# Triangles inverted as 64x64 blocks, a third set of a pair's prepared tiles, and another list of the weave

## The chip, the cores and the metric

The kernel runs on one core of one Trainium2 chip. The metric is the device time of one execution in microseconds (us); a time is the median of the timed executions. The core has a matrix engine (TensorE, PE in the rows), a vector engine (VectorE, DVE), a scalar engine (ScalarE, ACT), a general engine (GpSimd, POOL) and a sync engine (SP) that issues most of the transfers. Each engine works through a list of instructions of its own, in that list's order.

## What is computed

Two blocks of a model on 256 tokens of width 1024. The change touches one part of the first block, the RWKV-7 recurrence, which runs over the tokens in both directions. Beside it, in the same stage, stand an attention with eight heads and the output projection of both.

```python
def wkv7_scan(r, w, k, v, kk, a, reverse):          # per head: S is 64 x 64
    def step(state, inp):
        r_t, w_t, k_t, v_t, kk_t, a_t = inp
        sa = jnp.einsum('bhvk,bhk->bhv', state, -kk_t)
        state = (state * w_t[:, :, None, :]
                 + sa[..., :, None] * (kk_t * a_t)[..., None, :]
                 + v_t[..., :, None] * k_t[..., None, :])
        y = jnp.einsum('bhvk,bhk->bhv', state, r_t)
        return state, y

def first_block(...):
    mod = silu(c) @ ada_w + ada_b          # six modulation vectors
    ...
    att = dilated_mixture_attention(qa, ka, va).reshape(B, S, A)
    rw = rwkv7_bidirectional(...)          # wkv7_scan, forward and reversed, 8 heads
    mixed = jnp.concatenate([att, rw], axis=-1) @ w_out
    x = x + gate1 * mixed
    ...
```

## The kernel before

The recurrence is computed in chunks of 64 tokens. In a chunk the sequential steps are a triangular system, whose matrix is inverted by doubling: a triangle made of blocks is put together from inverses half as large, in five levels. What is left between chunks is a chain of 64x64 states.

Two heads make a **pair**, so there are four pairs, 0 to 3 (class `Pair`). A pair has two directions `d` and two halves `t` of the tokens; a half has two chunks of 64. For each pair five kinds of tasks are written as Python generators:

- `prepare` (its products stand at L606 to L670 of the profile) makes what the recurrence needs of a pair: `vn`, `na`, `nbk`, `ar`, `btk`, `az`, `bon`. The names come from the helpers `t1` and `t2`, which add `q % 2` to most of them, so that there are two sets of these tiles, used by pairs in turn.
- `start(d, t)` (L687) makes the chunk's products of tokens with tokens and masks them (L691, L693) into `PR`. `PR` holds, for two heads and two matrices, 128x128 matrices that are zero outside their two diagonal 64x64 blocks, one block for each chunk. `PB` is a copy for the last sums; it too has two sets.
- `tile(d, t)` is the inversion. GpSimd makes the first `X` (L708, L709) from `MA`, the system's matrix in `PR`. Each of five levels has two **half-levels**: two products with `MA` on TensorE (L720) and a multiplication with a mask, `PP`, on VectorE (L721), then two products with `PP` (L725), a transpose on VectorE (L727) and a copy on an engine that is free (L728). All of these are 128x128 for each head. Three products (L735, L743, L746) give `W`.
- `states` (L761 to L774) is the chain over the four chunks in both directions, and ends with 16 sums into `y` (L595, from `PB` and `W`).
- `finish` (L789 to L804) normalises `y` and writes the pair's output.

The function `weave` puts the tasks of the stage into one order: pairs 0 to 3, the eight attention heads (L522 to L553, one after the other, since all use one tile `bias`), the modulation vectors that are needed later (`ada`: VectorE's multiply-adds L341, 1024 KB of weights each load, and sums on TensorE at L345), and the output projection (`outs`: splits of the weights at L99 and L100, three products at L106 to L108, additions to x at L954). It keeps an estimate of when each engine is free and each task ready, takes the task that could start first, and among equals the one that stands first in the list. It starts when pair 0 is prepared; the other pairs' `prepare` stands in the list with what it must follow. `prepare` of pair q waits for all of `start` of pair q - 1 and for `finish` of pair q - 2, whose tiles it writes over:

```python
first.append((("pre", q), pairs[q].prepare(), tuple(("s", q - 1, d, t) for d in range(2) for t in range(2))
              + ((("fin", q - 2),) if q > 1 else ())))
```

Behind the weave stand the fourth pair's part of the output projection, a loop over the last weights that were loaded ahead (the first products at L106 from `zr` and `kk`), and then the rest of the first block and the second block.

Of the kernel before, what the change touches and what calls it, by code (L numbers as in the profile page):

```python
# [28 lines left out]
HALVES = slice(0, 64), slice(64, 128)  # L29
# [409 lines left out]
def masks(k, keep, pool):  # L439
# [10 lines left out]
    up = pool.tile([128, 128], F, name="up")  # L450
    nc.vector.tensor_tensor(up, pi, fi, op=OP.is_lt)
    lo = pool.tile([128, 128], F, name="lo")
    nc.vector.tensor_tensor(lo, pi, fi, op=OP.is_gt)
    m = keep.tile([128, 2, 8, 128], F, name="masks")
    t = pool.tile([128, 128], F, name="mt")
    for d, tri in enumerate((up, lo)):
        nc.vector.scalar_tensor_tensor(m[:, d, 6], xf, 64.0, tri, op0=OP.is_lt, op1=OP.mult)
        nc.vector.tensor_tensor(m[:, d, 7], m[:, d, 6], k.ident, op=OP.add)
        for i in range(6):
# [3 lines left out]
            nc.vector.tensor_tensor(m[:, d, i], m[:, d, i], k.ident, op=OP.add)  # L463
    k.masks = m
    k.bm = keep.tile([128, 128], F, name="bm")
    nc.vector.tensor_scalar(k.bm, xf, 64.0, None, op0=OP.is_lt)
# [103 lines left out]
class Pair:  # L570
# [8 lines left out]
    def t1(self, name):  # L579
        keep = name[:2] in ("vn", "na", "kd", "bo")  # L580
        return self.pool.tile([128, T], F, name=name + (str(self.q % 2) if keep else ""))

    def t2(self, name, shape):
        return self.pool.tile(shape, F, name=name + (str(self.q % 2) if name[:3] != "btk" else ""))
# [13 lines left out]
    def prepare(self):  # L598
# [75 lines left out]
        self.W, self.PB = [None] * 2, [[None] * 2 for _ in range(2)]  # L674

    def start(self, d, t):
# [4 lines left out]
        PR = self.blocks(pool, f"PR{d}{t}", [128, 2, 2, 2, 128])  # L681
# [7 lines left out]
        for x in range(2):  # L689
            for r in HALVES:  # L690
                nc.vector.tensor_tensor(PR[r, :, x, :, r], ps[x][r], up[r, None, 6:8, r].to_broadcast([64, 2, 2, 64]),  # L691
                                        op=OP.mult)
        nc.gpsimd.tensor_copy(self.PB[d][t], PR[:, :, 0, 1])  # L693

    def tile(self, d, t):
# [6 lines left out]
        bc = lambda x: x[:, None, :].to_broadcast([128, 2, 128])  # L702
        PR = k.zeroed[f"PR{d}{t}"]
        X = pool.tile([128, 2, 2, 128], F, name=f"X{d}{t}")
        pp = pool.tile([128, 2, 128], F, name=f"PP{d}{t}")
        MA = PR[:, :, 0, 0]

        nc.gpsimd.tensor_tensor(MA, MA, bc(k.ident), op=OP.add)  # L708
# [1412 lines left out]
```

## Time and profile before

| | us |
|---|---|
| median of 3 timed executions | 2327.96 (2327.71 to 2334.68) |
| the profiled execution | 2320.28 |
| its span, first to last instruction | 2318.2 |
| TensorE busy | 2191.8 (95% of the span) |
| VectorE busy | 1735.9 (75%) |
| ScalarE busy | 1264.6 (55%) |
| GpSimd busy | 809.6 (35%) |
| mean granted TensorE clock | 0.973 |

A row of a timeline tells when instructions of one kind started on an engine, for how long they ran, the line of the kernel, the operation, the tile written and the tiles read, the instruction's shape and how many rows like it were put together. Matrix products overlap, so the time from one start to the next is what one costs, and the time in the row is that with its latency. A row of a group tells the busy time in all, the mean ns of one, the idle time ahead of them, and what ended most of it. The granted clock is the share of full speed that TensorE was given.

### The profile page before, as it was taken

Reading aid. Unit: us, or ns where it says so; the run is one execution under the profiler, and the core shown is the slowest. Engines: PE = TensorE matmul, PEld = TensorE weight load, DVE = VectorE, ACT = ScalarE, POOL = GpSimd, SP = SyncE. Lnnn points to the kernel's source line nnn. Section 1 sums busy time; section 2 is a strip of 40 time slices with the busy share of each in tenths; the row PEclk is TensorE's granted clock in tenths of the full one; section 3 lists DMA queues with packets and bytes.
Section 4 is the critical chain, followed back from the end, with each engine's and each line's share of the span. In section 5 each row is a group of like instructions: output and inputs, shape, how many; then the busy total and the mean of one; then the engine's idle time right before and its main releaser. Section 6 shows DMA issues by size and latency. Waiting matters only on the chain.

```text
span 2318.2 us, 46849 instructions
## 1 busy us (share of the span) xinstructions
PE 2191.8 (95%) x17962; PEld 2079.0 (90%) x17962; DVE 1735.9 (75%) x3278; ACT 1264.6 (55%) x2689; POOL 809.6 (35%) x811
## 2 busy tenths in 40 slices
PE   6999898789899999999999999899999999989998
PEld 3878587789799999999999999878899999979998
DVE  6888886899877888777776765678875666777664
ACT  3543532735477776555554644447556666536543
POOL 1132320569877777444444100101432221131000
PEclk8999898899999999999999999999999999989999
DMA  7422123447655666666665675323565555516663
GB/s 266 149 92 86 61 73 96 119 107 173 162 148 155 154 150 177 196 196 195 193 193 165 185 219 193 122 74 111 155 202 166 181 162 191 178 36 192 190 200 119
DMA packets 304064, 358.38 MB, mean 155 GB/s; under 512 B 24188, under 2 KB 276576, under 8 KB 302816
## 3 DMA queue, kind: packets, MB, share of 16 engines
q1 hardware_dynamic: 291456, 349.53, 50.0%
q10 hardware_dynamic: 12384, 5.86, 1.0%
q8 instruction: 141, 2.31, 0.4%
q14 instruction: 83, 0.68, 0.1%
HBM read 354.28 MB, written 1.05 MB: 153 GB/s over the span
## 4 chain that ended last, share of the span: by engine, by line
PE 76%; DVE 13%; DMA 3%; ACT 3%; issue 2%; POOL 2%; SPq 0%; ACTq 0%; DVEq 0%; POOLq 0%
PE g L106 12%; PE g L108 12%; PE g L107 12%; PE o L106 4%; PE o L107 4%; PE o L108 3%; PE g L1162 2%; PE y L1314 2%; PE o L1314 2%; PE y L1312 2%; PE o L1312 2%; PE o L1313 2%; PE y L1313 2%; DVE uT L1001 2%; DVE wl L100 2%
## 5 line engine op out<-in xcount | busy, mean ns | idle before, releaser
L99 ACT ACTIVATE wh<-raw 128x1024 fp32r<-128x1024 f32 (+3 forms) x397 | 387.1, 977 | 389.2 <-PE g L107 185.5
L100 DVE TENSOR_TENSOR wl<-raw,wh 128x1024 fp32r<-128x1024 f32 (+3 forms) x381 | 431.6, 1135 | 223.2 <-ACT wh L99 209.8
L106 PE MATMUL g<-xh,wh 128*128 128x256 f32 x1864 | 529.9, 285 | 8.7 <-ACT xh L374 5.8
L108 PE MATMUL g<-xh,wl 128*128 128x256 f32 x1864 | 525.4, 282 | 8.4 <-DVE wl L100 8.3
L107 PE MATMUL g<-xl,wh 128*128 128x256 f32 x1864 | 524.6, 282 | 4.1 <-DVE xl L375 2.7
L1001 POOL TENSOR_TENSOR ul<-uT,uh 128x512 fp32r<-128x512 f32 x320 | 411.6, 1306 | 188.4 <-ACT uh L1001 188.4
L106 PEld LDWEIGHTS g<-xh,wh 128*128 128x128 f32 x1864 | 357.5, 192 | 15.2 <-ACT xh L374 6.9
L108 PEld LDWEIGHTS g<-xh,wl 128*128 128x128 f32 x1864 | 356.2, 191 | 12.1 <-DVE wl L100 11.7
L107 PEld LDWEIGHTS g<-xl,wh 128*128 128x128 f32 x1864 | 356.4, 191 | 6.1 <-DVE xl L375 3.5
L1001 ACT ACTIVATE uh<-uT 128x512 fp32r<-128x512 f32 x384 | 221.3, 627 | 146.5 <-POOL ul L1001 76.5
L108 PE MATMUL g<-ph,ul 128*128 128x256 f32 x1024 | 291.1, 284 | 7.7 <-POOL ul L1001 7.6
L106 PE MATMUL g<-ph,uh 128*128 128x256 f32 x1024 | 292.8, 286 | 3.7 <-ACT uh L1001 2.0
L107 PE MATMUL g<-pl,uh 128*128 128x256 f32 x1024 | 289.1, 282 | 0.0
L108 PEld LDWEIGHTS g<-ph,ul 128*128 128x128 f32 x1024 | 194.7, 190 | 11.3 <-POOL ul L1001 11.1
L106 PE MATMUL o<-hh,wh 128*128 128x256 f32 x704 | 197.8, 281 | 1.6 <-DVE t L1374 1.6
L106 PEld LDWEIGHTS g<-ph,uh 128*128 128x128 f32 x1024 | 195.1, 191 | 4.6 <-ACT uh L1001 2.3
L107 PE MATMUL o<-hl,wh 128*128 128x256 f32 x704 | 197.4, 280 | 0.0
L108 PE MATMUL o<-hh,wl 128*128 128x256 f32 x704 | 197.1, 280 | 0.0
L107 PEld LDWEIGHTS g<-pl,uh 128*128 128x128 f32 x1024 | 195.3, 191 | 0.0
L1001 DVE TENSOR_TENSOR al<-G,ah 128x256 fp32r<-128x256 f32 x128 | 173.9, 1359 | 17.2
L154 POOL TENSOR_TENSOR sql<-sq,sqh 128x256 fp32r<-128x256 f32 x48 | 48.8, 1018 | 340.1 <-ACT sqh L153 336.0
L1001 DVE STREAM_TRANSPOSE uT<-u 128x1024 f32<-128x1024 f32 x128 | 157.8, 1235 | 2.3 <-DMA u<-in_peer_u_dram 1.9
(772 smaller groups left out, 5456.4 us busy)
## 6 DMA issues: line engine op xcount, KB each, us to landing
u<-in_peer_u_dram SPq DMA_DIRECT2D x512, 128.0 KB, 2.6
raw<-in_ffn_w_gate_dram SPq DMA_DIRECT2D x44, 1024.0 KB, 5.6
raw<-in_ffn_w_up_dram SPq DMA_DIRECT2D x44, 1024.0 KB, 5.3
u<-in_peer_v_dram SPq DMA_DIRECT2D x64, 512.0 KB, 4.3
uT<-in_peer_v_dram SPq DMA_DIRECT2D x64, 512.0 KB, 4.2
raw<-in_ffn_w_down_dram SPq DMA_DIRECT2D x32, 1024.0 KB, 5.1
raw<-in_ada_w_dram SPq DMA_DIRECT2D x24, 1024.0 KB, 5.2
raw<-in_w_in_dram SPq DMA_DIRECT2D x13, 1024.0 KB, 5.7
```

What stands on the lines that cost most here:

```text
L99: nc.scalar.activation(h, v, AF.Copy)
L100: self.sub.tensor_tensor(l, v, h.bitcast(F), op=OP.subtract)
L106: nc.tensor.matmul(out, sh, mh, start=first, stop=False)
L107: nc.tensor.matmul(out, sh, ml, start=False, stop=False)
L108: nc.tensor.matmul(out, sl, mh, start=False, stop=last)
L154: self.sub.tensor_tensor(l, sq, h.bitcast(F), op=OP.subtract)
L1001: return lambda *args, **kw: self.tc.keep_in_program_order(f(*args, **kw))
L1162: nc.tensor.matmul(p[:, t], g[:, t], b[:, t], start=True, stop=True)
L1312: nc.tensor.matmul(o, vh[:, s], ah, start=i == 0 and c % 2 == 0, stop=False, skip_group_check=True)
L1313: nc.tensor.matmul(o, vh[:, s], al, start=False, stop=False, skip_group_check=True)
L1314: nc.tensor.matmul(o, vl[:, s], ah, start=False, stop=i == NB - 1, skip_group_check=True)
```

## The change

Three edits. The triangles are now stored as 64x64 blocks: the rows 0 to 63 of a tile hold one chunk's block and the rows 64 to 127 the other's, and the zero blocks are gone. A half-level is four products of 64x64 by 64, two heads times two diagonal quarters of TensorE, in place of two of 128x128 by 128. Masks, `PP`, `X`, transposes and copies are half as wide. `start` writes `PA` (two matrices in blocks) and `PR` (two with zeros, as before); the last level's result is put into `TT`, with zeros, in two copies. Second, `t1` and `t2` name three sets, and `prepare` of pair q waits for `finish` of q - 3; `start` of pair q now waits for `finish` of q - 2, since `PB` and `W` keep two sets. Third, the weave's list has the pairs' tasks first, then the heads, then the modulation.

```diff
     def t1(self, name):
         keep = name[:2] in ("vn", "na", "kd", "bo")
-        return self.pool.tile([128, T], F, name=name + (str(self.q % 2) if keep else ""))
+        return self.pool.tile([128, T], F, name=name + (str(self.q % 3) if keep else ""))
...
+        self.PA[d][t] = PA = pool.tile([128, 2, 2, 64], F, name=f"PA{d}{t}")
+        PR = self.blocks(pool, f"PR{d}{t}", [128, 2, 2, 128])
         self.PB[d][t] = pool.tile([128, 2, 128], F, name=f"PB{d}{t}{self.q % 2}")
...
         for x in range(2):
+            nc.vector.tensor_tensor(PA[:, x], ps[x][:, :, 0], up[:, 6, None].to_broadcast([128, 2, 64]), op=OP.mult)
+        for x in range(2):
             for r in HALVES:
-                nc.vector.tensor_tensor(PR[r, :, x, :, r], ps[x][r], up[r, None, 6:8, r].to_broadcast([64, 2, 2, 64]),
-                                        op=OP.mult)
-        nc.gpsimd.tensor_copy(self.PB[d][t], PR[:, :, 0, 1])
+                nc.vector.tensor_tensor(PR[r, x, :, r], ps[x][r, :, 1], up[r, 7, None].to_broadcast([64, 2, 64]), op=OP.mult)
+        nc.gpsimd.tensor_copy(self.PB[d][t], PR[:, 0])
...
+        ic = [(i, r) for i in range(2) for r in HALVES]
...
         for lv in range(1, 6):
             yield
-            p = k.pw([128, 2, 128])
-            for i in range(2):
-                nc.tensor.matmul(p[:, i], MA[:, i], X[:, 1, i], start=True, stop=True)
+            p = k.pw([128, 2, 64])
+            for i, r in ic:
+                nc.tensor.matmul(p[r, i], MA[r, i], X[r, 1, i], start=True, stop=True)
             nc.vector.tensor_mul(pp, p, bc(lo[:, lv]))
             yield
-            p = k.pw([128, 2, 128])
-            for i in range(2):
-                nc.tensor.matmul(p[:, i], pp[:, i], X[:, 0, i], start=True, stop=True)
+            p = k.pw([128, 2, 64])
+            for i, r in ic:
+                nc.tensor.matmul(p[r, i], pp[r, i], X[r, 0, i], start=True, stop=True)
             if lv < 5:
                 nc.vector.transpose(X[:, 1], p)
-            nc.any.tensor_copy(X[:, 0], p)
+                nc.any.tensor_copy(X[:, 0], p)
+        for r in HALVES:
+            nc.any.tensor_copy(tt[r, :, r], p[r])
...
-                                  + ((("fin", q - 2),) if q > 1 else ())))
+                                  + ((("fin", q - 3),) if q > 2 else ())))
...
                     first.append((("s", q, d, t), pairs[q].start(d, t), ((("pre", q),) if q else ())
-                                  + (((q - 1, d, t),) if q else ())))
+                                  + (((q - 1, d, t),) if q else ()) + ((("fin", q - 2),) if q > 1 else ())))
...
-            weave(nc, ada + heads + first + last + outs + [("ow", last_weights(), ("oa", ("pre", 3)))])
+            weave(nc, first + last + heads + ada + outs + [("ow", last_weights(), ("oa", ("pre", 3)))])
```

The order of instructions moves with it. In what follows a row is the line, the operation, the tile written, the tiles read and how many of the kind follow each other; `x4` of 64x64 is one half-level.

TensorE in the first level of pair 0, before. L720 and L725 are half-levels, L546 and L552 an attention head, L654, L659 and L614 pair 1's `prepare`.

```order
L720 MATMUL o_1717<-X_1635,PR_1581 128x128 x2
L546 MATMUL g_1721<-ident,sc 128x128 x4
L552 MATMUL g_1731<-bias,vna 64x256 x2
L659 MATMUL g_1749<-ident,ar_1703 128x128 x2
L720 MATMUL g_1753<-X_1639,PR_1590 128x128
L654 MATMUL o_1742<-ident,btk_1710 128x128 x4
L720 MATMUL g_1753<-X_1639,PR_1590 128x128
L725 MATMUL o_1757<-X_1635,PP_1636 128x128 x2
```

The same place now (L735 and L740 are the half-levels, L663 and L668 `prepare`).

```order
L735 MATMUL g_1726<-X_1642,PA_1580 64x64 x4
L735 MATMUL o_1732<-X_1648,PA_1590 64x64 x4
L735 MATMUL g_1738<-X_1654,PA_1607 64x64 x4
L740 MATMUL g_1744<-X_1642,PP_1643 64x64 x4
L740 MATMUL o_1751<-X_1648,PP_1649 64x64 x4
L740 MATMUL g_1758<-X_1654,PP_1655 64x64 x4
L663 MATMUL g_1766<-ident,btk_1712 128x128 x4
L668 MATMUL o_1773<-ident,ar_1705 128x128 x2
```

Half-levels of three tiles follow each other directly, and no attention head stands between them.

TensorE around `finish` of pair 0 and `start` of pair 2, now (L807, L812 and L818 are `finish`, L698 is `start`; L750 to L761 are the products for `W` of pair 1).

```order
L807 MATMUL o_2642<-y,bm 128x256
L740 MATMUL g_2646<-X_2102,PP_2103 64x64 x4
L735 MATMUL g_2653<-X_2366,PA_2270 64x64 x4
L750 MATMUL g_2670<-vn_1674,PA_2072 64x64 x4
L812 MATMUL o_2659<-sq,bm 128x256
L740 MATMUL g_2676<-X_2366,PP_2367 64x64 x4
L758 MATMUL o_2687<-PP_2103,TT_1656 128x64 x2
L761 MATMUL o_2687<-TT_1656,na_1772 64x128 x2
L818 MATMUL g_2693<-lora_378,gup 128x256
L698 MATMUL g_2698<-az_1128,btk_2340 64x256 x2
L698 MATMUL o_2699<-az_1128,btk_2340 64x256 x2
```

Before, pair 2's `prepare` (L606, L614) stood behind the last product of pair 0's `finish` (L803), and 38 rows lay between that and its `start`.

```order
L803 MATMUL g_2523<-lora_372,gup 128x256
L606 MATMUL g_2527<-ident,zr_369 128x128 x2
L614 MATMUL g_2535<-lora_371,wda 128x256
L720 MATMUL g_2539<-X_2192,PR_1620 128x128 x2
L743 MATMUL o_2517<-PP_2133,X_2132 128x64 x2
```

Now `start` itself stands directly behind it, and pair 2's `prepare` ahead.

TensorE behind the last pair's sums, before.

```order
L595 MATMUL y_3244<-PB_3360,W_3629 64x128 x2
L595 MATMUL y_3244<-PB_3220,W_3629 64x128 x2
L792 MATMUL g_4081<-y,bm 128x256
L803 MATMUL g_4096<-lora_372,gup 128x256
L797 MATMUL o_4085<-sq,bm 128x256
L106 MATMUL g_4109<-zr_4105,kk 128x256
L107 MATMUL g_4109<-zr_4106,kk 128x256
```

The same place now (L536, L555 and L561 are attention heads, L345 the modulation).

```order
L604 MATMUL y_3281<-PB_3464,W_3697 64x128 x2
L604 MATMUL y_3281<-PB_3247,W_3697 64x128 x2
L555 MATMUL o_3977<-ident,sc 128x128 x4
L807 MATMUL g_3984<-y,bm 128x256
L561 MATMUL o_4005<-bias,vna 64x256 x2
L812 MATMUL g_3988<-sq,bm 128x256
L345 MATMUL g_3999<-one,acc 128x1 x4
L818 MATMUL g_4012<-lora_378,gup 128x256
L536 MATMUL g_4019<-qk_385,qk_381 128x256 x2
L555 MATMUL o_4040<-ident,sc 128x128 x4
L561 MATMUL g_4048<-bias,vna 64x256 x2
L345 MATMUL g_4055<-one,acc 128x1 x4
```

Before, the loop over the last weights (L106) followed `finish`; now heads 4 to 7, the last five of the modulation's eight groups and 168 products of the output projection stand between.

VectorE in one of these heads, now (L538, L541, L542, L548, L550 and L562 are the head's steps, L341 the modulation's multiply-adds).

```order
L538 TENSOR_TENSOR sc<-g_4111,bias 128x512
L341 SCALAR_TENSOR_TENSOR acc<-raw,ct,acc 128x512
L541 TENSOR_REDUCE smx<-sc 128x2
L341 SCALAR_TENSOR_TENSOR acc<-raw,ct,acc 128x512
L542 TENSOR_SCALAR smx<-smx 128x2
L341 SCALAR_TENSOR_TENSOR acc<-raw,ct,acc 128x512 x2
L548 RECIPROCAL sden<-sden 128x2
L341 SCALAR_TENSOR_TENSOR acc<-raw,ct,acc 128x512
L550 TENSOR_SCALAR sc<-sc,sden 128x256 x2
L562 COPY att<-g_4140 64x256
```

Before, the recurrence's steps stood between the steps of a head.

## Rows read from the trace of the kernel before

**Rows 1.** Busy us by stretch (instructions) of each engine, clock, DMA share, GB/s

```profile
240.00:300.00 60.00, 49.59 (x323) 36.84 (x323) 53.00 (x140) 29.05 (x70) 24.01 (x24) 0.89 0.14 45
...
372.00:400.00 28.00, 22.73 (x141) 17.53 (x140) 15.16 (x40) 5.08 (x11) 0.00 (x0) 0.81 0.34 107
sum 260.00, PE 237.53 PEld 191.84 DVE 218.95 ACT 102.20 POOL 64.50; mean PE 59.38 PEld 47.96 DVE 54.74 ACT 25.55 POOL 16.12
```

**Rows 2.** Timeline of TensorE, half-levels and a head: start us, us, instruction

```profile
301.47 0.71 PE L720 MATMUL g<-X,PR 128*128 128x128 f32 x4
302.02 0.61 PE L720 MATMUL o<-X,PR 128*128 128x128 f32 x4
302.47 1.06 PE L720 MATMUL g<-X,PR 128*128 128x128 f32 x8
303.36 0.60 PE L670 MATMUL o<-kd,bm 128*128 128x256 f32 x2
303.79 0.38 PE L725 MATMUL g<-X,PP 128*128 128x128 f32 x2
```

**Rows 3.** Timeline of TensorE, two products of a start

```profile
307.85 0.60 PE L687 MATMUL o<-az,btk 128*64 128x256 f32 x4
308.28 0.60 PE L687 MATMUL g<-az,btk 128*64 128x256 f32 x4
```

**Rows 4.** Timeline of TensorE, two products in a prepare

```profile
279.27 0.48 PE L614 MATMUL o<-lora,wda 64*128 64x256 f32 x1
279.27 0.48 PE L614 MATMUL g<-lora,wda 64*128 64x256 f32 x1
```

**Rows 5.** Timeline of TensorE in the second block

```profile
1501.45 0.28 PE L106 MATMUL g<-xh,wh 128*128 128x256 f32 x1
1501.56 0.28 PE L107 MATMUL g<-xl,wh 128*128 128x256 f32 x1
1501.76 0.29 PE L1523 MATMUL o<-cg,w 64*64 64x15 f32 x4
1501.98 0.60 PE L119 MATMUL o<-one,R 1*128 1x1 f32 x4
```

**Rows 6.** Groups of VectorE, 140 to 350 us: busy us, mean ns | idle before

```profile
L341 DVE SCALAR_TENSOR_TENSOR acc<-raw,ct,acc 128x512 f32<-128x512 f32 x44 | 34.1, 775 | 0.1
L721 DVE TENSOR_TENSOR PP<-g,masks 128x256 f32<-128x256 f32 x49 | 19.9, 412 | 4.2 <-PE g L720 3.5
L727 DVE STREAM_TRANSPOSE X<-g 128x256 f32<-128x256 f32 x39 | 16.5, 432 | 2.5 <-PE g L725 2.4
...
L532 DVE TENSOR_REDUCE smx<-sc 128x2 f32<-128x512 f32 x8 | 5.3, 668 | 0.0
...
L772 DVE TENSOR_TENSOR st<-sn,g 128x128 f32<-128x128 f32 x10 | 2.7, 275 | 1.3 <-PE g L768 1.2
```

**Rows 7.** Timeline of TensorE: pair 0's sums, pair 2's prepare and start

```profile
226.14 1.04 PE L595 MATMUL y<-PB,W 128*64 128x128 f32 x16
...
233.85 0.38 PE L606 MATMUL g<-ident,zr 128*128 128x128 f32 x2
...
258.23 0.65 PE L687 MATMUL o<-az,btk 128*64 128x256 f32 x4
```

**Rows 8.** Groups of GpSimd, 140 to 350 us

```profile
L522 POOL TENSOR_SCALAR bias<-df 128x512 f32<-128x512 f32 x7 | 11.7, 1676 | 38.5 <-PE g L552 38.4
L523 POOL TENSOR_TENSOR bias<-bias,lc 128x512 f32<-128x512 f32 x8 | 10.9, 1358 | 0.3
```

**Rows 9.** Groups of ScalarE, 140 to 350 us

```profile
L537 ACT ACTIVATE sc<-sc,smx 128x256 f32<-128x256 f32 x16 | 8.0, 500 | 3.6 <-DVE smx L533 3.5
L548 ACT COPY bias<-g 128x512 f32<-128x512 f32 x6 | 3.5, 586 | 7.9 <-PE g L546 7.9
```

**Rows 10.** The chain that ended last, 387 to 411 us: start us, us, what

```profile
389.39 2.39 PE y L595 x18
...
399.92 0.58 PE g L106
```

More of the change, by code (lines that the diff above doesn't have):

```diff
@@ L449, in masks @@
     nc.vector.tensor_copy(xf, xi)
[L450 to L455, printed above, removed]
+    k.bm = keep.tile([128, 128], F, name="bm")
+    nc.vector.tensor_scalar(k.bm, xf, 64.0, None, op0=OP.is_lt)
+    pc = pool.tile([128, 64], I32, name="pc")
+    nc.vector.tensor_scalar(pc, pi[:, 0:64], 63, None, op0=OP.bitwise_and)
+    fc = fi[:, 0:64]
+    xi, xf = xi[:, 0:64], xf[:, 0:64]
+    nc.vector.tensor_tensor(xi, pc, fc, op=OP.bitwise_xor)
+    nc.vector.tensor_copy(xf, xi)
+    up = pool.tile([128, 64], F, name="up")
+    nc.vector.tensor_tensor(up, pc, fc, op=OP.is_lt)
+    lo = pool.tile([128, 64], F, name="lo")
+    nc.vector.tensor_tensor(lo, pc, fc, op=OP.is_gt)
+    m = keep.tile([128, 2, 8, 64], F, name="masks")
+    k.unit = keep.tile([128, 64], F, name="unit")
+    nc.vector.tensor_tensor(k.unit, pc, fc, op=OP.is_equal)
+    t = pool.tile([128, 64], F, name="mt")
     for d, tri in enumerate((up, lo)):
-        nc.vector.scalar_tensor_tensor(m[:, d, 6], xf, 64.0, tri, op0=OP.is_lt, op1=OP.mult)
-        nc.vector.tensor_tensor(m[:, d, 7], m[:, d, 6], k.ident, op=OP.add)
+        nc.vector.tensor_copy(m[:, d, 6], tri)
+        nc.vector.tensor_tensor(m[:, d, 7], tri, k.unit, op=OP.add)
         for i in range(6):
@@ L462, in masks @@
             nc.vector.scalar_tensor_tensor(m[:, d, i], xf, 2 * b, t, op0=OP.is_lt, op1=OP.mult)
-            nc.vector.tensor_tensor(m[:, d, i], m[:, d, i], k.ident, op=OP.add)
+            nc.vector.tensor_tensor(m[:, d, i], m[:, d, i], k.unit, op=OP.add)
     k.masks = m
-    k.bm = keep.tile([128, 128], F, name="bm")
-    nc.vector.tensor_scalar(k.bm, xf, 64.0, None, op0=OP.is_lt)
 def selectors(k, pool):
@@ L580, in t1 @@
         keep = name[:2] in ("vn", "na", "kd", "bo")
-        return self.pool.tile([128, T], F, name=name + (str(self.q % 2) if keep else ""))
+        return self.pool.tile([128, T], F, name=name + (str(self.q % 3) if keep else ""))
     def t2(self, name, shape):
-        return self.pool.tile(shape, F, name=name + (str(self.q % 2) if name[:3] != "btk" else ""))
+        return self.pool.tile(shape, F, name=name + (str(self.q % 3) if name[:3] != "btk" else ""))
     def blocks(self, pool, name, shape):
@@ L673, in prepare @@
         self.yp = None
-        self.W, self.PB = [None] * 2, [[None] * 2 for _ in range(2)]
+        self.W, self.PB, self.PA = [None] * 2, [[None] * 2 for _ in range(2)], [[None] * 2 for _ in range(2)]
     def start(self, d, t):
@@ L701, in tile @@
         up, lo = m[:, d], m[:, 1 - d]
[L702 to L708, printed above, removed]
+        bc = lambda x: x[:, None, :].to_broadcast([128, 2, 64])
+        PR, PA = k.zeroed[f"PR{d}{t}"], self.PA[d][t]
+        X = pool.tile([128, 2, 2, 64], F, name=f"X{d}{t}")
+        pp = pool.tile([128, 2, 64], F, name=f"PP{d}{t}")
+        tt = self.blocks(pool, f"TT{d}{t}", [128, 2, 128])
+        MA = PA[:, 0]
+        ic = [(i, r) for i in range(2) for r in HALVES]
+        nc.gpsimd.tensor_tensor(MA, MA, bc(k.unit), op=OP.add)
         nc.gpsimd.tensor_tensor(X[:, 0], MA, bc(up[:, 0]), op=OP.mult)
@@ L714, in tile @@
             r = slice(64 * i, 64 * i + 64)
[L715 removed]
+            self.ymm(i, self.yp[r, t * 128:(t + 1) * 128], self.vn[:, t, r], PR[:, 1, i])
         for lv in range(1, 6):
             yield
[L718 to L720 removed]
+            p = k.pw([128, 2, 64])
+            for i, r in ic:
+                nc.tensor.matmul(p[r, i], MA[r, i], X[r, 1, i], start=True, stop=True)
             nc.vector.tensor_mul(pp, p, bc(lo[:, lv]))
             yield
[L723 to L725 removed]
+            p = k.pw([128, 2, 64])
+            for i, r in ic:
+                nc.tensor.matmul(p[r, i], pp[r, i], X[r, 0, i], start=True, stop=True)
             if lv < 5:
                 nc.vector.transpose(X[:, 1], p)
[L728 removed]
+                nc.any.tensor_copy(X[:, 0], p)
+        for r in HALVES:
+            nc.any.tensor_copy(tt[r, :, r], p[r])
         yield
[L730 to L731 removed]
+        z0 = pp.rearrange("p i t -> p (i t)")
         p = k.pw([128, 128])
[L733 to L735 removed]
+        for i, r in ic:
+            nc.tensor.matmul(p[r, HALVES[i]], PA[r, 1, i], self.vn[r, t, HALVES[i]], start=True, stop=True)
         nc.any.tensor_copy(z0, p)
```

7 lines of the change are left out of this document (removed).

## The prediction, made before the changed kernel was timed

> **What bounds the kernel now.** I read the busy time by stretches first, then the single rows of the stretch that the change rewrites, then the order of both kernels there. The part in question runs from 140 us, where the first pair's `start` opens the weave, to 399.9 us, where the loop over the last weights opens [rows 1, 10]. In these 260 us TensorE is busy for 237.5 and VectorE for 219.0 (84%); ScalarE (102) and GpSimd (64) bound nothing [rows 1]. There are two weak places. Between 240 and 300 us TensorE is busy for 49.6 of 60 us at a mean granted clock of 0.89, since pair 2 can't start: pair 0's last sums are issued at 226.1, pair 2's `prepare` begins only at 233.9, behind pair 0's `finish`, and its `start` comes at 258.2 [rows 7]. And from 372 on the last pair's states run as a chain of single steps: the clock is at 0.81 and VectorE is busy for 15 of 28 us [rows 1]. What lies behind 400 us is the same code in both kernels, and what lies ahead of 140 loses some mask columns on VectorE while the start waits for weights; I cost both at nothing.
>
> **The change, part by part.**
>
> *Levels of the inversion on TensorE.* There are 16 tiles x 5 levels x 2 = 160 half-levels. Each was two products of 128x128 by 128 columns, which the trace shows as four instructions; now it is four of 64x64 by 64 columns, or eight instructions, which alternate between the two diagonal quarters of the array. Before, one takes 302.47 - 302.02 = 0.45 us from start to start [rows 2]. For the new form the trace has bounds only. If the quarters take turns: four instructions with 64x64 weights, all in one quarter, took 0.22 us, 0.055 each [rows 5], and eight make 0.44, no gain. If the two quarters run at once: 0.22. Halves do run at once here in two rows. Four instructions of 256 columns into the two halves of the output take 0.43 us [rows 3], as long as two do on the whole array [rows 2]; and two products from the two halves of the input start at the same 279.27 us [rows 4]. No row shows the diagonal. I take 0.22, since a diagonal differs in both halves: 160 x 0.23 = 37 us less on TensorE. It comes back in part: a half-level behind other work costs some 0.1 us more (0.55 us from 301.47 to 302.02, against 0.45 [rows 2]), and the new order has about 73 runs of half-levels between instructions of other shapes, so + 7.
>
> *One tile for both quarters.* The two quarters of a half-level write the upper and the lower partitions of one tile `p`; the two products of [rows 4], which start together, write two tiles, `o` and `g`. So no row shows two halves of the input that write one tile at once. If they can't, a half-level takes 0.44 us and not 0.22; that is rival A. The Trainium skill (TensorEngine Tiling (Array Packing), Restrictions and Gotchas) says that different row tiles can't access the same PSUM bank simultaneously, and by that rule A is the case.
>
> *VectorE.* 80 mask products go from 256 to 128 columns: 0.41 us now [rows 6], 0.275 for a product of that width from PSUM [rows 6]; the transposes (64 between levels, 16 ahead of them) from 0.43 to some 0.29. That is 160 x 0.135 = 21.5 us less. `start` has six products of about 0.28 for four of 0.42, the same sum. ScalarE's copies and GpSimd's two steps per tile halve too; neither engine is on the path.
>
> *The third set.* `prepare` of pair 2 now needs `start` of pair 1 and no `finish`. That takes away the wait of [rows 7]: up to the 24 us between 233.9 and 258.2, for pair 2 and again for pair 3. But `PB` and `W` still have two sets, so `start` of pair q now waits for `finish` of q - 2. The order has pair 0's last `finish` product directly ahead of pair 2's `start`. The wait isn't gone, it is shortened to the sums and the four steps of `finish`, while pair 1's levels have TensorE.
>
> *The list.* With the recurrence first, TensorE's order holds attention heads 0 to 2 and the scores of head 3 inside the recurrence; heads 4 to 7, five of the eight modulation groups and all of the out-projection come behind it. So the stage falls into two parts, which I sum apart.
>
> Part I, 140 us to the last sums of pair 3. By TensorE: 237.5, less 168 products of the out-projection at 0.115 [rows 5] = 19.4, less 4.3 heads of (0.86 + 0.45 + 0.86, by the distances of [rows 2]) = 9.3, less some 5 for the sums of five modulation groups (an estimate), less 37, plus 7: 174, so an end at 314 if TensorE never idles; with half of the 22 us that it idles now, 325. By VectorE: 219, less 40 multiply-adds of modulation at 0.775 = 31, less 4.3 heads at 2.3 (add and maximum at 0.67 [rows 6] and five small steps of 0.2) = 10, less 16 splits and 16 adds of the out-projection at 0.67 and 0.41 (by rows of equal width [rows 6]) = 17, less pair 3's `finish`, some ten steps of 0.28, 3, less 21.5, plus 1 for new copies: 137, and at today's 84% 163, so an end at 303. I take 313: the first 35 us (one pair's levels alone) are bound by the chain of steps and the rest by TensorE, and the low-clock stretches go with the wait.
>
> Part II, from there to the loop over the last weights. It is a chain, since the heads share one `bias` tile, which GpSimd fills only when the head before has read it. One head: bias 1.68 + 1.36 on GpSimd [rows 8], add and maximum 0.67 each [rows 6], two exponentials at 0.5 and the copy 0.59 [rows 9], four transposes 0.61 and the product 1.06 with their latency [rows 2], and six small steps (negation, two sums, reciprocal, two scalings), narrower than the 0.28 of [rows 6], at an estimated 0.2 each: 8.8. Between the steps VectorE's order has multiply-adds of the next modulation group: three of the eight lie ahead of a step that is ready, 3 x 0.775 = 2.3; three lie under GpSimd's bias and two under the exponentials. With ten hand-overs between engines, an estimated 0.8 in all, this is 12 us. The loads of modulation weights that the order has in a head fit under it. Head 3's rest 3, heads 4 to 7 48, the last head's two copies 1.3. Then the out-projection: 168 x 0.115 = 19.4 on TensorE, while VectorE has 17 + 12 multiply-adds at 0.775 = 26; I take 24, since the second half has none of them. Sum: 76.3.
>
> 313 + 76.3 = 389 against 399.9: **11 us less**. The profiled execution took 2320.3 us (span 2318.2); against the median of 2328.0 the same difference gives **2317 us**.
>
> **Rivals.**
>
> A. *The quarters take turns* (ends on the other side). A half-level stays at 0.44, and the new switches stay. Of the 37 us the part that TensorE bounds is behind the first pair, three quarters: + 27. 313 becomes 340, the loop over the last weights starts at 416, 16 us later than now: **2344 us**. It decides from 0.22 + 11 / 120 = 0.31 us a half-level. For it: one tile, and no row with a diagonal. Against it: [rows 3] has two output halves of one tile written at once, and the diagonal's halves share neither input nor output lines.
>
> B. *The tail eats the gain.* Today's attention costs nothing, because it lies beside the levels; in part II TensorE works for about 3 us in 12, and at half the clock, as in the stretch from 372 on [rows 1], a head's transposes and products take 1.3 us more; a late weight load stops VectorE's queue, and the scalings behind it, for another 0.7, about one multiply-add. Four heads then take 56, the out-projection 26.6: + 10.6, and the stage ends where it does now: **2328 us**, no change. For it: every step of the chain is in order. Against it: a share of one head is still beside pair 3's states.
>
> C. *Part I follows VectorE*, 303: 22 us less, **2306 us**. For it: 84% is what VectorE holds over the whole stage [rows 1]. Against it: 314 by TensorE's sum alone.
>
> D. *The wait for `finish` two pairs back replaces the one removed in full*: pair 2 starts 8 us later than the sum supposes, the time from 226.1 to 233.9 in [rows 7], and pair 3 as well; half is filled with pair 1's levels: + 8, **2325 us**.
>
> **How the numbers follow.** The forecast (0.22 us, 12 us a head) has 0.42, A 0.22, B 0.18, C 0.10, D 0.08. About 0.3%, 7 us, is what a measurement of this kernel tells from no change. The forecast's own range is 2308 to 2325, 0.37 of it below 2321; with C that makes 0.47 for faster. B and D and the forecast's upper end make 0.25 for no change; A, with the upper end of B, 0.28 for slower. The range reaches from C with a shorter tail, 2302, to A with some of B on top, 2346; left out are A with all of B and a gain over 1.1%.
>
> **What would show it.** A half-level: the distance from start to start of the new 64x64 rows of lines 735 and 740 where several follow each other, 0.22 or 0.44 us. VectorE's rows of 128x128 at 0.28 to 0.30. Pair 2's `start` near 210 us (258 now), pair 3's sums ending near 313 (some 9 us ahead of 399.9 now), with no stretch below a clock of 0.9 between 180 and 300. Behind it four heads 12 us apart, GpSimd's bias to GpSimd's bias, with a low granted clock, then 24 us of out-projection, and the loop over the last weights at 389. The prediction is wrong if the quarters take turns, if heads lie over 14 us apart, or if part I ends outside 303 to 325.

## The result: slower by 0.9%, and the profile after

The changed kernel takes 2353.2 us (median of 6, 2343.7 to 2358.2) against 2330.1 (median of 6): a ratio of 1.0088, 95% interval 1.0065 to 1.0111, some 20 us slower. 2317 was forecast. The profiled execution took 2354.8 us. It lies 1.6 us above its median and that of before 10 us below its own, so some 11 of the 34 us between the two profiles are not the change. All that follows is read from the stage itself, from the first `start` to the loop over the last weights: 289 us now (141.8 to 430.9), 260 before (140.3 to 399.9).

Busy time by stretches of the kernel after: the recurrence up to pair 3's last sums, the heads behind it, the output projection (columns as in [rows 1]).

```profile
141.80:344.10 202.30, 182.56 (x2132) 134.52 (x2132) 149.68 (x482) 75.04 (x210) 41.82 (x69) 0.87 0.06 20
344.10:403.00 58.90, 30.93 (x103) 19.89 (x103) 37.94 (x74) 15.24 (x36) 11.02 (x8) 0.56 0.46 149
403.00:430.90 27.90, 24.77 (x178) 23.69 (x178) 21.94 (x41) 8.82 (x15) 0.10 (x1) 0.89 0.42 138
```

Part I, forecast to take 173 us, takes 202, and part II 87 in place of 76. A mean clock of 0.87 is some 51 us at the lower level, 1.2 GHz, in part I. They lie in six stretches, two of them of 17 us, the others of 3 to 7. The first long one, in windows of 2 us:

```profile
196.00:198.00 2.00, 1.55 (x30) 1.11 (x26) 2.00 (x6) 1.08 (x3) 0.74 (x1) 1.00 0.03 8
198.00:200.00 2.00, 0.80 (x6) 0.62 (x6) 2.00 (x8) 1.14 (x3) 0.00 (x0) 1.00 0.00 0
200.00:202.00 2.00, 2.00 (x19) 1.11 (x20) 0.62 (x3) 1.74 (x6) 0.00 (x0) 0.77 0.00 0
202.00:204.00 2.00, 2.00 (x27) 1.88 (x26) 1.42 (x5) 1.34 (x5) 0.00 (x0) 0.50 0.00 0
...
218.00:220.00 2.00, 2.00 (x30) 1.37 (x28) 1.03 (x4) 0.10 (x1) 1.92 (x2) 0.96 0.00 0
```

VectorE is busy without a gap from 196 to 200, nearly all of it with pair 2's `prepare`, TensorE waits 1.65 us for its `btk`, and just behind that the clock falls and stays at 0.50 until 218, though TensorE is busy all the time. The same comes back at 249 to 266 with pair 3's `prepare`, where the wait is 1.27 us. Before, heads and modulation stood in these places.

The half-level itself is what was forecast. TensorE's timeline at the full clock (x8 is one half-level; each of its four products is two instructions):

```profile
314.75 0.45 PE L740 MATMUL o<-X,PP 64*64 64x64 f32 x8
315.03 0.40 PE L735 MATMUL g<-X,PA 64*64 64x64 f32 x8
315.26 0.40 PE L750 MATMUL o<-vn,PA 64*64 64x64 f32 x8
...
317.21 0.44 PE L761 MATMUL g<-TT,na 128*64 128x128 f32 x4
317.57 0.45 PE L735 MATMUL g<-X,PA 64*64 64x64 f32 x8
317.95 0.48 PE L807 MATMUL o<-y,bm 128*128 128x256 f32 x1
```

From 315.03 to 315.26 is 0.23 us. The eight instructions behind that row start in pairs, 0.007 us apart in a pair and 0.058 from pair to pair, so the two quarters run at once, though they write one tile. The Trainium skill (TensorEngine Tiling (Array Packing), Restrictions and Gotchas) says that different row tiles can't access one PSUM bank simultaneously; the measurement decides, and by it rival A falls. Alone between other shapes a half-level takes 317.95 - 317.57 = 0.38 us, 0.15 more, where 0.1 was put.

The heads behind the recurrence, by GpSimd's first step of each, which opens a head:

```profile
346.84 1.49 POOL L531 TENSOR_SCALAR bias<-df 128x512 f32<-128x512 f32 x1 [13.07 <-PE o L561]
361.32 1.49 POOL L531 TENSOR_SCALAR bias<-df 128x512 f32<-128x512 f32 x1 [11.64 <-PE g L561]
374.47 1.49 POOL L531 TENSOR_SCALAR bias<-df 128x512 f32<-128x512 f32 x1 [10.31 <-PE g L561]
388.60 1.49 POOL L531 TENSOR_SCALAR bias<-df 128x512 f32<-128x512 f32 x1 [11.29 <-PE g L561]
```

They lie 14.5, 13.2 and 14.1 us apart; 12 was forecast. VectorE's timeline in one of them:

```profile
362.99 0.16 DVE L346 TENSOR_TENSOR mod<-g,V 128x4 f32<-128x4 f32 x1 [3.85 <-PE g L345]
363.08 1.37 DVE L339 TENSOR_SCALAR acc<-raw,ct 128x512 f32<-128x512 f32 x1
364.48 0.75 DVE L341 SCALAR_TENSOR_TENSOR acc<-raw,ct,acc 128x512 f32<-128x512 f32 x1
365.15 0.68 DVE L538 SCALAR_TENSOR_TENSOR sc<-g,bias 128x512 f32<-128x512 f32 x1
365.75 0.74 DVE L341 SCALAR_TENSOR_TENSOR acc<-raw,ct,acc 128x512 f32<-128x512 f32 x1
366.41 0.68 DVE L541 TENSOR_REDUCE smx<-sc 128x2 f32<-128x512 f32 x1
367.00 0.74 DVE L341 SCALAR_TENSOR_TENSOR acc<-raw,ct,acc 128x512 f32<-128x512 f32 x1
367.66 0.16 DVE L542 TENSOR_SCALAR smx<-smx 128x2 f32<-128x2 f32 x1
367.78 1.54 DVE L341 SCALAR_TENSOR_TENSOR acc<-raw,ct,acc 128x512 f32<-128x512 f32 x2
369.23 0.16 DVE L548 RECIPROCAL sden<-sden 128x2 f32<-128x2 f32 x1
369.35 0.75 DVE L341 SCALAR_TENSOR_TENSOR acc<-raw,ct,acc 128x512 f32<-128x512 f32 x1
370.02 0.61 DVE L550 TENSOR_SCALAR sc<-sc,sden 128x256 f32<-128x256 f32 x2
```

Heads and modulation are one chain here. VectorE waits 3.85 us for the sums of the modulation on TensorE (L345), which stand behind the last head's product; then seven of a group's eight steps (L339, L341) stand ahead of the head's scaling (L550), some 5.5 us. Not all of that lengthens the head, since the first of them lie beside GpSimd's bias and two beside the exponentials; how much it does is read from g2 below. TensorE's transposes and last product in the same head:

```profile
370.42 1.16 PE L555 MATMUL o<-ident,sc 128*128 128x128 f32 x4 [5.47 <-DVE sc L550]
372.34 1.97 PE L561 MATMUL g<-bias,vna 128*64 128x256 f32 x4 [0.75 <-ACT bias L557]
```

The clock is at 0.5 here. The prediction had 0.61 and 1.06 for them, at the full clock, so 1.5 us of the head are the clock's. In the output projection TensorE stands still once, behind a split that waits for a load of weights:

```profile
416.09 0.57 PE L106 MATMUL g<-qk,wh 128*128 128x256 f32 x1 [2.92 <-ACT wh L99]
```

### The profile page after: what moved, and what is told of

It reads as the page before. It is cut to its first block, busy times and chain, and to the rows that moved or that the text cites. A ratio compares the mean times of both kernels' runs of the same rounds, so it can differ in the third digit from the quotient of the medians.

```text
span 2353.0 us, 48360 instructions
## 1 busy us (share of the span) xinstructions
PE 2196.0 (93%) x18666; PEld 2066.7 (88%) x18666; DVE 1723.1 (73%) x3331; ACT 1261.7 (54%) x2691; POOL 797.1 (34%) x815
## 4 chain that ended last, share of the span: by engine, by line
PE 75%; DVE 13%; DMA 3%; issue 3%; POOL 2%; ACT 2%; SPq 0%; ACTq 0%; DVEq 0%; POOLq 0%
PE g L106 12%; PE g L108 12%; PE g L107 11%; PE o L106 3%; PE o L107 3%; PE o L108 3%; PE g L1177 2%; PE y L1327 2%; PE o L1327 2%; PE o L1328 2%; PE y L1328 2%; PE o L1329 2%; PE y L1329 2%; DVE uT L1016 2%; DVE wl L100 2%
## 5 line engine op out<-in xcount | busy, mean ns | idle before, releaser
L106 PE MATMUL g<-xh,wh 128*128 128x256 f32 x1864 | 530.1, 285 | 5.5 <-ACT xh L374 2.7
L106 PEld LDWEIGHTS g<-xh,wh 128*128 128x128 f32 x1864 | 356.6, 192 | 11.7 <-ACT xh L374 3.3
L106 PE MATMUL g<-ph,uh 128*128 128x256 f32 x1024 | 292.5, 286 | 3.4 <-ACT uh L1016 1.9
L106 PE MATMUL o<-hh,wh 128*128 128x256 f32 x704 | 197.6, 281 | 1.6 <-DVE t L1389 1.6
L106 PEld LDWEIGHTS g<-ph,uh 128*128 128x128 f32 x1024 | 195.2, 191 | 4.4 <-ACT uh L1016 2.3
```

The costliest lines, as they stand in the source:

```text
L106: nc.tensor.matmul(out, sh, mh, start=first, stop=False)
```

## The three edits apart

Each kernel is given by its edit against the kernel before or after; ratios are to the kernel before, with 95% intervals.

**e1_blocks_third_oldlist**: the kernel after with the list of before.

```diff
-            weave(nc, first + last + heads + ada + outs + ...
+            weave(nc, ada + heads + first + last + outs + ...
```

> The changed kernel with the list of before (modulation, heads, then the recurrence); blocks and third set stay. Theory L (the list costs the time: without heads and modulation in it, TensorE idles in the recurrence behind VectorE, its granted clock falls to 0.5 for 18 us twice, and the heads left over stand alone behind it at 0.5): faster than before by 8 to 20 us, about 2315, and the loop over the last weights opens near 385 us of the profile; between the first start and that loop TensorE is at 0.5 for less than 25 us. Theory B (the 64x64 products cost it, since a half-level between products of other shapes takes 0.38 us and not 0.23, and TensorE's load falls): no faster than before, 2330 or more, and the clock falls here too.

Measured: 2339.3 us, 1.0032 (1.0018 to 1.0047). **e2_blocks_only** takes the sets and waits of before as well (`q % 3` to `q % 2`, `fin` of q - 2 for `prepare`, none for `start`).

> The kernel before with the 64x64 blocks alone: two sets, the waits and the list of before. Theory L: faster than before by some 5 to 12 us, 2320; a half-level takes 0.23 us behind another and some 0.35 elsewhere, where it took 0.45. Theory B: 2330 to 2345, with more low clock than before's 16 us between 240 and 300.

Measured: 2332.6 us, 1.0019 (0.9999 to 1.0038). **e3_list_only** is the kernel before with the new list.

> The kernel before with the new list alone: 128x128 products, two sets. Theory L: slower than before by 15 to 30 us, 2345 to 2360, with heads at 13 to 14 us each behind the recurrence at a clock of 0.5 to 0.6. Theory B: within 7 us of before, 2330.

Measured: 2377.8 us, 1.0206 (1.0183 to 1.0229). **e4_third_only** is the kernel before with three sets and their waits.

> The kernel before with the third set alone (prepare of pair q waits for finish of q - 3, start of pair q for finish of q - 2), 128x128 products and the old list. Theory L: 0 to 8 us faster, 2326: pair 2's prepare comes ahead of pair 0's finish, and the 16 us at a low clock between 240 and 300 shrink, but start still waits for that finish. Theory B makes no other forecast here; if this is slower than before by over 5 us, the third set is a cause of its own.

Measured: 2327.8 us, 0.9984 (0.9972 to 0.9997). **g4_blocks_newlist_two_sets** is the kernel after without the third set.

> The changed kernel (2353 us) without the third set: blocks and the new list, two sets, prepare of pair q behind finish of q - 2 again. If the third set brings what the new list costs less with it (e3_list_only 2378 against 2353 for all three), this takes 2365 to 2378; if the blocks bring it, 2350 to 2358.

Measured: 2358.0 us, 1.0132 (1.0105 to 1.0158), at the upper end of its second case.

So the list costs 2.1% on the kernel before, and still 0.6% with the other two edits (1.0032 to 1.0088). The third set brings 0.2% in the old list with 128x128 products and nothing there with the blocks (e2 to e1); in the new list it brings some 0.4%, but the intervals of g4 and the kernel after overlap. The blocks bring 0.7% under the new list (e3 to g4), but nothing under the old one (0.2% slower with two sets, 0.5% with three). The first part of theory L held, its forecast for e1 and e2 missed, and theory B's was met: narrow products don't pay even with the list of before. The stage of the kernel before and that of e1 show why one may suspect the clock:

```profile
140.30:399.90 259.60, 237.16 (x1705) 191.74 (x1704) 218.56 (x549) 102.20 (x258) 64.20 (x77) 0.94 0.23 73
143.10:419.30 276.20, 244.82 (x2410) 181.14 (x2409) 196.92 (x579) 96.08 (x274) 52.06 (x79) 0.80 0.22 70
```

0.80 in 276 us is 110 us at the lower level; before it was 0.94 in 260, or 31 us. And in e1 it falls where TensorE has no gap at all:

```profile
190.00:192.00 2.00, 2.00 (x29) 1.47 (x27) 1.69 (x4) 0.41 (x2) 0.13 (x1) 1.00 0.01 4
192.00:194.00 2.00, 2.00 (x24) 1.68 (x23) 1.19 (x7) 1.34 (x6) 0.58 (x2) 1.00 0.87 208
194.00:196.00 2.00, 2.00 (x14) 1.27 (x12) 1.96 (x7) 0.48 (x3) 0.66 (x2) 0.66 0.85 325
196.00:198.00 2.00, 2.00 (x10) 1.22 (x6) 0.62 (x3) 0.00 (x0) 0.00 (x0) 0.50 0.00 0
```

## Is it the clock, or the changes of shape?

**h1_wide_quarters** keeps the number of e1's instructions, the order of its tasks and the quarters of the array, and lets each product stream both heads' columns, twice as many; half of the result is not used. TensorE's list is the same but for some 150 instructions, nearly all of which moved by fewer than 20 places.

```diff
-            p = k.pw([128, 2, 64])
+            p = k.pw([128, 4, 64])
             for i, r in ic:
-                nc.tensor.matmul(p[r, i], MA[r, i], X[r, 1, i], start=True, stop=True)
+                nc.tensor.matmul(p[r, 2 * i:2 * i + 2], MA[r, i], X[r, 1], start=True, stop=True)
+            p = p[:, 0:4:3]
```

(the second half-level likewise; the weave counts the products as before).

> The kernel of e1_blocks_third_oldlist (2339 us) with the order of its tasks kept, and each of the four products of a half-level streaming 128 columns, both heads' blocks, where one head's 64 are used: as many instructions, on the same quarters of the array, twice the columns, so 0.45 us where 0.23 stood, 36 us more of TensorE's work. Clock theory: the clock is 1.0 but for 20 to 40 us of the stage, and the time falls below e1's by 8 to 20 us, to 2319 to 2331. Theory of shapes: the clock is a by-product, and the kernel is slower than e1 by 10 to 30 us, 2350 to 2370.

Measured: 2324.5 us, 0.9992 (0.9977 to 1.0007), 15 us **faster** than e1 with 36 us more of TensorE's work. Its stage:

```profile
141.50:398.20 256.70, 234.35 (x2409) 177.34 (x2408) 198.17 (x583) 98.27 (x271) 52.25 (x79) 0.99 0.23 75
```

The clock is at 0.99. Worked out: e1 loses half of 110 us to it, h1 half of 7 (one stretch, at 152); 51 us regained less 36 of work is 15, and the stage is 19.5 us shorter. This shows that the clock eats the blocks' gain under the old list. Why narrow products bring the clock down no run shows.

**h3_wide_quarters_two_sets** does the same to e2.

> e2_blocks_only (2333 us), order of its tasks kept, with 128 columns for each of a half-level's products as in h1. Clock theory: clock above 0.93 in the stage where e2 has 0.84, and 2315 to 2328. Theory of shapes: 2345 to 2365.

Measured: 2328.1 us, 1.0003 (0.9990 to 1.0016), stage 264 us at a clock of 0.93 where e2 has 267 at 0.84: the same way, but smaller, and in the time not clear of the noise.

**f2_whole_array_oldlist** goes the other way: 64 columns, on the whole array.

```diff
-            for i, r in ic:
-                nc.tensor.matmul(p[r, i], MA[r, i], X[r, 1, i], start=True, stop=True)
-            nc.vector.tensor_mul(pp, p, bc(lo[:, lv]))
+            for i in range(2):
+                nc.tensor.matmul(p[:, i], MP[:, i], X[:, 1, i], start=True, stop=True)
+            for r in HALVES:
+                nc.vector.tensor_mul(pz[r, :, r], p[r], bc(lo[:, lv])[r])
```

(the second half-level likewise, with `pz`; GpSimd fills `MP`. The weave counts the new work, so the order of tasks moves.)

> As e1_blocks_third_oldlist (2339 us), but a half-level is two products of 128x128 by 64 columns: the weights stand in zero-padded tiles (MP by two GpSimd copies a tile, PZ by two VectorE products of 64 partitions in place of one, some 0.27 us more for each of 80), the columns stay in blocks. TensorE's time for a half-level is 0.22 us again by its columns. Theory C: the whole array works, and the clock holds better than in e1 (mean above 0.90 between 150 and 320 us, where e1 has about 0.73); VectorE's 20 us come back, so 2322 to 2335. Theory S: the shape doesn't change between a half-level and its 128x128 neighbours, so less is lost there too, but the clock in e1's places is as low as it was: 2335 to 2345.

Measured: 2442.7 us, 1.0485 (1.0462 to 1.0509); both theories missed it by 100 us. Its stage, and two half-levels in a run:

```profile
139.00:519.00 380.00, 357.81 (x1744) 288.96 (x1743) 224.37 (x649) 97.19 (x271) 65.15 (x118) 0.60 0.14 44
```

```profile
166.56 1.06 PE L745 MATMUL o<-X,PZ 128*128 128x64 f32 x4
167.41 1.06 PE L739 MATMUL g<-X,MP 128*128 128x64 f32 x4
```

The clock is at 0.60 over 380 us with TensorE busy for 94% of them. A half-level takes 0.85 us there, and half of that, 0.43, would be no less than the 0.45 that 128 columns take in [rows 2]; my 0.22 for it was wrong as well.

**f1_filler_oldlist** puts one unused product of 128x128 by 128 ahead of each half-level of e1, **h2_filler_every_other** ahead of the first of each level. In h2 the order of the tasks is e1's; in f1 the weave counts the fillers, and the order moves too.

```diff
             p = k.pw([128, 2, 64])
+            nc.tensor.matmul(p.rearrange("p i t -> p (i t)"), k.bm, k.ident, start=True, stop=True)
             for i, r in ic:
```

> Blocks, third set and the list of before (the kernel of e1_blocks_third_oldlist, 2339 us), and ahead of each half-level one product more, 128x128 by 128 of two constants, into the tile that the half-level then writes over: work without a use, some 0.22 us each at the full clock, 36 us in all. Theory C (what eats the blocks' gain is the granted clock: TensorE was at 0.5 for about 100 us of e1's stage, though the profile has it busy nearly all the time): with the filler the clock stays at 1.0 but for some 20 us, and the time falls below e1's by 8 to 20 us, to 2320 to 2331, though TensorE has more to do. Theory S (the half-levels between other shapes cost it, 0.38 us each and a late start for their neighbours; the clock is a by-product): the filler adds 10 to 36 us, 2350 to 2375.

> e1_blocks_third_oldlist (2339 us), order of its tasks kept, with the filler of f1 ahead of the first half-level of each level alone (80 products of 128x128 by 128, some 0.25 to 0.45 us each with the change of shape, 20 to 36 us). Clock theory: the clock holds for most of the stage (mean above 0.90, where e1 has 0.80) and the time falls to 2320 to 2335. Theory of shapes: 2350 to 2365.

Measured: 2359.1 us, 1.0147 (1.0113 to 1.0181), and 2347.9, 1.0102 (1.0083 to 1.0121): slower than e1 by 20 and 9 us, f1 in the range of the theory of shapes, h2 just below it. Their stages were at 0.96 in 286 us and 0.89 in 284, so the clock did come back (44 and 24 us regained by the sum used for h1), and the fillers cost more than that: 54 us for 160, 32 for 80, or 0.34 to 0.40 each, where their columns alone are 0.22. By this sum a change of shape has a price of 0.1 to 0.2 us; h1, which has no more of them than e1, is the clean comparison.

**i1_wide_first_half_level** and **i2_wide_second_half_level** stream the double columns in one half-level of two.

> h1_wide_quarters (2324.5 us) with 128 columns in the first half-level of each level alone and 64 in the second, order of the tasks kept: 18 us less of TensorE's work than h1. If the clock holds (0.97 or more in the stage) and TensorE bounds it: 2310 to 2320, faster than before by 0.3 to 0.7%. If the clock falls for a part, between e1 and h1: 2325 to 2338.

> As i1, with 128 columns in the second half-level of each level and 64 in the first. By the clock theory no different from i1 by more than 5 us: 2310 to 2320 if the clock holds, 2325 to 2338 if it falls for a part.

Measured: 2327.0 us, 1.0009 (0.9983 to 1.0036), and 2330.3, 1.0007 (0.9993 to 1.0022). i1's executions run from 2317.5 to 2352.1 us. The profiled ones, 2345.9 and 2338.7 us and so among the longer, have 0.88 and 0.87 between 140 and 410 us: the double columns in one half-level of two don't hold the clock dependably.

## What sets the new list's time

**h4_wide_quarters_newlist** is the kernel after with h1's edit.

> The changed kernel (2353 us), its order kept, with 128 columns for each of a half-level's products as in h1. Clock theory: the stretches at 0.5 at 201 to 219 and 249 to 268 us go, the last sums of pair 3 come 0 to 15 us ahead of 344 though TensorE has 36 us more to do, the tail stays: 2338 to 2353. Theory of shapes: the sums come 15 to 35 us later, 2368 to 2390.

Measured: 2357.2 us, 1.0115 (1.0095 to 1.0136). Part I:

```profile
140.60:346.40 205.80, 195.00 (x2132) 146.39 (x2132) 150.94 (x486) 74.30 (x206) 42.62 (x69) 0.96 0.06 19
```

The two stretches of 17 us are gone and the clock comes back, 0.87 to 0.96, which is 18 us regained; 36 us of work are added, and TensorE's idle time falls from 20 to 11. By this sum part I is 9 us longer, measured are 3.5, and the time can't be told from that of the kernel after; both forecasts missed. So under the new list the clock takes back about half of what the narrow columns save, and idle time about a quarter.

**f3_filler_newlist** is the kernel after with f1's filler.

> The changed kernel (2353 us) with the same filler ahead of each half-level. Theory C: the two stretches at 0.5 in the recurrence (about 201 to 219 and 249 to 268 us) shrink or go, the last pair's sums end 5 to 15 us ahead of 344, the tail stays as it is at a clock near 0.56: 2338 to 2348. Theory S: the sums end 10 to 30 us later, 2363 to 2380.

Measured: 2408.6 us, 1.0335 (1.0300 to 1.0369). The clock was at 1.0 from 158 us on, fell at 243, after TensorE had stood still for 1.4 us of the last 3, and stayed at 0.5 for 82 us, in which it was busy throughout. The order of tasks moves here as in f1. Theory C is refuted here in its form "filler holds the clock"; what kept it low for so long stays open.

**f4_filler_in_heads** has fillers in heads 4 to 7 alone.

> The changed kernel (2353 us) with filler products (128x128 by 128 of constants) in attention heads 4 to 7 alone: 6 ahead of a head's scores, 8 ahead of its transposes, 2 ahead of its last product, into tiles that are then written over. TensorE waits there for other engines, so at the full clock they cost little. If the low clock is what makes a head 14 us and not 12 (transposes 1.18, scores 2.0, last product 1.97 us at 0.5), the clock rises above 0.8 between 344 and 403 us, a head takes 11 to 12.5 us and the time falls by 5 to 12 us, 2341 to 2348. If the chain over VectorE (multiply-adds between the head's steps) sets it, heads stay at 13.5 to 14.5 us: 2350 to 2358.

Measured: 2348.6 us, 1.0082 (1.0061 to 1.0103), not to be told from the kernel after. The clock rose, the heads did not get shorter:

```profile
344.90:428.90 84.00, 68.10 (x406) 57.26 (x407) 57.39 (x114) 24.35 (x52) 11.60 (x9) 0.85 0.47 151
```

```profile
365.32 1.98 POOL L531 TENSOR_SCALAR bias<-df 128x512 f32<-128x512 f32 x1 [14.57 <-PE g L567]
379.88 1.49 POOL L531 TENSOR_SCALAR bias<-df 128x512 f32<-128x512 f32 x1 [11.23 <-PE g L567]
394.49 1.49 POOL L531 TENSOR_SCALAR bias<-df 128x512 f32<-128x512 f32 x1 [11.78 <-PE g L567]
```

14.6 us each. This doesn't show that the clock is without effect. In the head of 379.88 the transposes take 0.66 us and the last product 1.08, less by 1.4 than at 0.5; but the transposes start only at 391.86, behind fillers and the next head's scores, where the scaling had ended at 390.0. What the rows gain the fillers take back.

**g2_modulation_first** puts the modulation into the recurrence, **g1_heads_before_recurrence** the heads.

```diff
-            weave(nc, first + last + heads + ada + outs + ...
+            weave(nc, ada + first + last + heads + outs + ...       (g2)
+            weave(nc, heads + first + last + ada + outs + ...       (g1)
```

> The changed kernel (2353 us) with modulation, the recurrence, heads and the output projection in this order: modulation inside the recurrence, four heads and the output projection behind it. If a tail head is long because the modulation's multiply-adds and sums stand in its chain, it takes 8.5 to 10.5 us here where it took 14, and the time falls to 2330 to 2345. If a head is 13 us or longer without them as well, the chain is the head's own: 2350 or more.

> The changed kernel (2353 us) with another list: heads, then the recurrence, then modulation and the output projection. All eight heads then stand inside the recurrence in TensorE's order and only the modulation and the output projection behind it. Theory T (a tail of heads is what the list costs: 59 us between 344 and 403 for four heads, with VectorE's multiply-adds and the sums of the modulation in one chain with them): the tail falls from 87 to 30 to 40 us, the recurrence grows by 5 to 15 us, and the kernel takes 2315 to 2330. Theory C2 (the clock of the narrow products in the recurrence decides whatever the list is, as in e1_blocks_third_oldlist at 2339): no better than that, 2335 to 2345, with 90 us or more at 0.5.

Measured: g2 2377.3 us, 1.0218 (1.0191 to 1.0244); g1 2357.8, 1.0128 (1.0104 to 1.0151). g2's heads:

```profile
393.45 1.49 POOL L531 TENSOR_SCALAR bias<-df 128x512 f32<-128x512 f32 x1 [9.16 <-PE g L561]
...
403.75 1.49 POOL L531 TENSOR_SCALAR bias<-df 128x512 f32<-128x512 f32 x1 [7.47 <-PE g L561]
...
414.05 1.49 POOL L531 TENSOR_SCALAR bias<-df 128x512 f32<-128x512 f32 x1 [7.46 <-PE g L561]
```

10.3 us each without the modulation between their steps, at a clock of 0.5. So of the 13.2 and 14.1 us of the kernel after's heads at that clock the modulation makes 2.9 and 3.8. But the time that the tail loses comes back in the recurrence: its part I takes 240 us at a clock of 0.76. In g1 all heads lie in the recurrence, which takes 226 us (0.84), and the output projection with the modulation takes 62 behind it; forecasts of 2315 to 2345 missed for both. **g3_third_heads_first** is g1's list with 128x128 products and the third set.

> 128x128 products, as before, with the third set (e4_third_only, 2328 us), and the list heads, recurrence, modulation, output projection. Theory T: the recurrence ends earlier than e4's 395 us but the output projection, which lay in it, comes behind: 2325 to 2345. With the clock at 1.0 there and narrow products at 0.5 in g1, theory C2 has this faster than g1 by 5 us or more; theory T has g1 faster, since it has 37 us less of TensorE's work.

Measured: 2343.2 us, 1.0070 (1.0049 to 1.0092), 15 us faster than g1, as the theory of the clock has it, though the products' shapes differ as well: its recurrence, heads included, takes 227 us with 128x128 products at a clock of 0.95, as long as g1's with half the columns. None of these lists reaches that of before: each leaves something that had lain beside the recurrence standing alone behind it. No version tried is faster than before by more than 0.3%; e4, the best, is by 0.16%.

## Why the prediction was wrong, step by step

- **A half-level, 0.22 us**: right in a run (0.23). Rival A falls. The 0.055 us for an instruction in one quarter came from rows of 15 columns, not of 64 [rows 5]; the 0.058 from pair to pair agrees with it. The change of shape was put at 0.1 and is 0.15.
- **VectorE**: mostly right. The mask product takes 0.287 us (0.275 put), the transpose 0.31 (0.29), and VectorE is busy for 150 us in part I against 137 put. It isn't the bound, so rival C falls (whose gain, by its own terms, is 21 us and not 22).
- **TensorE's sum for part I, 174 us and no more**: the step that failed. The work was right: 182.6 us busy less the 25 that the low clock added is 157, and the forecast's 174, which starts from 237.5 us with some 15 lost to the clock in them, is 159 without those. What was wrong is "the low-clock stretches go with the wait", and an idle time of nothing: 25 us of clock and 20 of idle time come on the work, 202 in all. 8 of the 20 lie in the first 38 us, where the first pair's chain is alone. I had read the low clock of [rows 1] as a thing of the wait for pair 2 alone, and priced narrower products at the full clock. That narrow products themselves bring the low clock is shown by h1 against e1 under the list of before and, for 18 of the 25 us, by h4 under the new one.
- **The third set**: right in kind. Pair 2's `prepare` begins at 192.8 us in place of 233.9 [rows 7], its `start` at 229.6 in place of 258.2; 210 was forecast. It comes 5 us behind pair 0's last sums, so rival D's wait is there, and short. Most of the lateness lies ahead of it: pair 0's sums are issued from 222.3 to 224, only some 3 us earlier than before, and the clock is at 0.5 from 201 to 218.
- **A head, 12 us**: 14, and so 8 us on four heads. The chain without modulation was sized well: 8.8, 0.8 for hand-overs and rival B's 1.3 for the half clock make 10.9, and g2 has 10.3. The forecast itself had the heads at a low clock ("What would show it"), but priced them at the full one: 1.5 us a head. The modulation was put at 2.3 us and makes 2.9 to 3.8. The out-projection takes 28 us for 24, and 2.9 of that is TensorE's wait for weights. With 87 for 76, rival B was right in its amount (10.6) and in the clock that it named; its late weight load comes in the out-projection and not in the heads, where modulation stands in its place.
- **The list**: in the sum only as its two parts, never held against the list of before, in which heads, modulation and out-projection lay beside the recurrence. What that was worth e3 shows: 2.1%, some 48 us. The tail that the new list lays bare costs more than the shorter recurrence brings: 202 and 87 us now stand where 260 stood.

Behind the stage the profile after is 4 us longer (1922 us from the loop on, 1918 before). The kernels of this study lie between 1914 and 1929 there, with the same code, so I take it for chance.

## What to carry to other kernels

A saving in TensorE's columns is worth its time only if the granted clock stays: read the clock of the stretch before pricing narrower products, and test by adding columns back. A planner's list that puts a chain first takes the filler out of it: look at what then stands alone behind it, and price that as a chain with all that its engines have queued between its steps.

## What had not been expected of the hardware

- Doubling the columns of 160 half-levels made the kernel 15 us faster (2339.3 to 2324.5), with the clock at 0.99 for 0.80.
- The granted clock fell from 1.0 to 0.5 in e1 at 195 us after TensorE had been busy for all of the time since 190; so busy time in the profile doesn't tell that the clock is safe.
- Products of 128x128 by 64 columns left TensorE at a mean clock of 0.60 for 380 us while it was busy 94% of the time (f2).
- Two quarters of the array that write the upper and the lower half of one tile run at once: 0.23 us for eight instructions, in pairs that start 0.007 us apart.
